# A hybrid decoder trunk on one core: the second token half's attention scores as three rounded products instead of one fp32 product

## The chip, the cores and the metric

The kernel runs on one core of one Trainium2 chip. A core has a matrix engine (PE; its weight loads are listed apart as PEld), a vector engine (DVE), an activation engine (ACT), a general engine (POOL), a queue engine (SP) and 16 DMA engines. Operands lie in SBUF, 128 partitions wide; matrix products land in PSUM, here in tiles of 128 x 512 fp32. The metric is the device time of one execution in microseconds. Three runs of the kernel before gave 992.62, 994.24 and 994.83 us, median 994.24.

## The reference

One sequence of 256 tokens, model width 2048, two layers. The first is a Mamba-2 mixer, the second an attention mixer; each is followed by `x = layernorm(alpha * x + mixer(x))`. The change lies in the second one, cut here to what matters:

```python
proj = x @ w_in                                   # [q | gate], each 2048 wide
q = (proj[..., :Q_WIDTH] + q_bias)                # 4 key-value heads x 8 query heads x 64
q = rope_partial(q, cos, sin)                     # first 16 of 64 dimensions
s = einsum("bcqhrd,bckhd->bchrqk", qb, kk) * (64 ** -0.5)
s = where(valid, s, -inf)                         # causal, window of 128
m = maximum(max(s), sink)
p = exp(s - m); p = p / (sum(p) + exp(sink - m))
o = einsum("bchrqk,bckhd->bcqhrd", p, vv) * silu(gate)
return o @ w_out
```

All inputs are fp32. With a window of 128, the first 128 tokens look at 128 keys, the second 128 tokens at 256. Keys and values are projected once, from the first layer's output.

## The kernel before, in words

**Products.** Nearly every product is made of three. A value a is split into a rounded part aH (type fp32r, which PE multiplies in one pass) and a remainder aL = a - aH; a product a b is then aH bH + aL bH + aH bL, summed in PSUM. For weights, ACT makes the rounded part (`wh`, L143) and DVE the remainder (`wl`, L144) of each half unit of 128 x 1024 that SP's queue has brought in (`wr`, L132). A unit is 128 x 2048 weights; PE spends 24 products of 512 columns or 48 of 256 on one. A few small products are plain fp32: among them the attention scores, L994.

**The first layer** (up to about 657 us) has its order written by hand. The change does not touch it.

**The attention layer** is written without a fixed order: a planner puts each engine's instructions into a queue by their place in the program and by when it reckons their inputs to be ready. On the chip, each engine then goes through its queue in order. The units come in the order `B_ORDER`: for each key-value head j a query block of four units (`q_block`, PE lines L881 to L883) and a gate block of four (`gate_block`, L269 to L271), later with the output blocks (`out_unit`, L330 to L332) between them. Small steps of attention are put off by a count of units with `later(n, fn)` and run by `tick()`.

For one head j the steps are these, h being the token half:

- `q_block` (L920): PE projects; DVE adds the bias row (L931) and rotates the first dimensions (`rope`, L862); DVE turns 32 x 32 blocks (L936), POOL's DMA queue writes them to DRAM and reads them back turned (`qd`, `qr`, L977 and L943).
- `scale_q` (L945): ACT copies the turned queries to `qT`, times 0.125.
- `attend` (L983): PE makes the scores L994, in fp32. Head dimension is 64, so two query heads use the two row halves of the PE array (rows 0 to 63 and 64 to 127), each into a PSUM tile of its own. For h = 0 there are 128 keys and two PSUM tiles, for h = 1 256 keys and four, of the four that the tag `ax` has. DVE takes the first half's scores out of PSUM (L1007); for the second half ACT copies and DVE fills in (L1002, L1003). Then come maximum, exponentials, sum and division (L1011 to L1022).
- `turn_p`, `load_p`: DVE turns the probabilities (L1028), POOL's queue writes and reads them (`pd`, `pT`). `mask_p` (L1042): for h = 1, DVE makes a masked copy `pm`. `pv` (L1048): PE multiplies with the values (L1052), DVE gates (`o`, L1059), ACT and DVE split the result (`oH` L1068, `oL` L1069).

The second half of head j follows one unit behind its first half. The masked copy of head j - 1, the query copy of head j and the scores of head j follow one another within some three units.

```python
for what, j in B_ORDER[:-1]:
    if what == "q":
        q_block(j)
        later(6, lambda j=j: attend(j, 0))
    elif what == "g":
        gate_block(j)
    else: ...
```

Of the kernel before, what the change touches and what calls it, by code (L numbers as in the profile page):

```python
# [8 lines left out]
F32 = mybir.dt.float32  # L9
F32R = mybir.dt.float32r  # L10
I32 = mybir.dt.int32
AF = mybir.ActivationFunctionType
ALU = mybir.AluOpType
AX = mybir.AxisListType

P = 128
S = 256
# [45 lines left out]
def trunk(ctx: ExitStack, tc: tile.TileContext, A: dict, out: bass.AP, dbg=None):  # L63
    nc = tc.nc
    PSUM = bass.MemoryType.PSUM

    def pool(name, bufs=1, side=None, space=None, stack=ctx):
        kw = {"space": space} if space is not None else {}
        return stack.enter_context(
            tc.tile_pool(name=name, bufs=bufs, side=side, reuse_waits="tile", **kw)  # L70
        )
# [9 lines left out]
    def nm(s):  # L81
        uid[0] += 1
        return f"{s}_{uid[0]}"

    def mm_tile():
        return mm_ps.tile([P, 512], F32, tag="mm", name=nm("mm"), bufs=4)
# [175 lines left out]
    def next_unit():  # L262
        used[0] += 1
        fill_units()
        flush()
        return units[used[0] - 1]
# [8 lines left out]
    def later(n, fn):  # L275
        pending.append([n, fn])
# [482 lines left out]
    for g in range(NG):  # L759
        t = 10 * g  # L760
# [92 lines left out]
    bp = pool("bp")  # L853
# [1 line left out]
    nc.gpsimd.dma_start(snk, A["snk"].partition_broadcast(P))  # L855

    def bias_row(src):
        t = bp.tile([P, 512], F32, tag="bias", name=nm("bias"), bufs=2)
        nc.gpsimd.dma_start(t[:], src.partition_broadcast(P))
        return t  # L860

    def rope(v, h, n):  # L862

        c = cs[:, h : h + 1, :].to_broadcast([P, n, 8])
        s = sn[:, h : h + 1, :].to_broadcast([P, n, 8])
        t = bp.tile([P, 4, 8, 8], F32, tag="rt", name=nm("rt"), bufs=1)
        x1, x2 = v[:, :, 0:8], v[:, :, 8:16]
        a, b, d, e = [t[:, i, :n, :] for i in range(4)]
        nc.vector.tensor_tensor(a, x1, c, ALU.mult)
        nc.vector.tensor_tensor(b, x2, s, ALU.mult)  # L870
        nc.vector.tensor_tensor(d, x2, c, ALU.mult)
        nc.vector.tensor_tensor(e, x1, s, ALU.mult)
        nc.vector.tensor_tensor(x1, a, b, ALU.subtract)
        nc.vector.tensor_tensor(x2, d, e, ALU.add)

    def x_stat(ps, h, u, ui):
        for k in range(4):
# [8 lines left out]
    kT = bp.tile([P, 4, S], F32, tag="kT", name="kT")  # L886
# [3 lines left out]
    for h in range(2):  # L890
        ps = mm_tile()
        for ui in range(4):
            if h == 0:
                kv_u.append(next_unit())
            x_stat(ps, h, kv_u[ui], ui)
        kd = bp.tile([P, 4, 2, 64], F32, tag="qt", name=nm("kd"), bufs=2)
        nc.vector.tensor_tensor(
            kd[:, :, 0, :], ps[:, :256].rearrange("p (j d) -> p j d", j=4),
            kvb[:, :256].rearrange("p (j d) -> p j d", j=4), ALU.add,
        )  # L900
        nc.vector.tensor_tensor(vt[:, h, :], ps[:, 256:], kvb[:, 256:], ALU.add)
        rope(kd[:, :, 0, :], h, 4)
        nc.gpsimd.tensor_copy(kd[:, :, 1, :], kd[:, :, 0, :])

        def ktr(h=h, kd=kd):
            pt = ax_tile()
            for j in range(4):
                nc.tensor.transpose(
                    pt[:, j * P : (j + 1) * P], kd[:, j, :, :].rearrange("p a d -> p (a d)"), ident
                )  # L910
            nc.scalar.copy(kT[:, :, h * P : (h + 1) * P], pt[:].rearrange("p (j t) -> p j t", j=4))

        later(2, ktr)
    nc.vector.tensor_tensor(vt[:, 1, :], vt[:, 1, :], vt[:, 0, :], ALU.subtract)

    qT = {}
# [3 lines left out]
    def q_block(j):  # L920
        pss = [mm_tile(), mm_tile()]
        qb = bias_row(A["qb"][j * 512 : (j + 1) * 512])
        for ui in range(4):
            u = next_unit()
            for h in range(2):
                x_stat(pss[h], h, u, ui)
            tick()
        for h in range(2):
            qt = bp.tile([P, 8, 64], F32, tag="qt", name=nm("qt"), bufs=2)
            qf = qt[:].rearrange("p a d -> p (a d)")  # L930
            nc.vector.tensor_tensor(qf, pss[h][:], qb[:], ALU.add)  # L931
            rope(qt[:], h, 8)

            def turn_q(h=h, qf=qf):
                z = bp.tile([P, 1024], F32, tag="pb", name=nm("zq"), bufs=5)[:, :512]
                nc.vector.transpose(  # L936
                    z.rearrange("p (c a t) -> p a c t", c=4, a=4), qf.rearrange("p (a c d) -> p a c d", a=4, c=4)
                )
                d = to_dram(z, 128, "qd")

                def load_q():
                    t = bp.tile([P, 8, 4, 32], F32, tag="pb", name=nm("qr"), bufs=5)[:, :4]
                    nc.gpsimd.dma_start(t.rearrange("p b a t -> p b (a t)"), d[:].rearrange("b p f -> p b f"))  # L943

                    def scale_q():  # L945
                        q2 = bp.tile([P, 4, P], F32, tag="qT", name=nm("qT"), bufs=2)
                        nc.scalar.activation(
                            q2[:].rearrange("p a (b t) -> p a b t", b=4), t.rearrange("p b a t -> p a b t"),
                            AF.Copy, scale=0.125,
                        )  # L950
                        qT[j, h] = q2

                    later(4, scale_q)

                later(1, load_q)

            turn_q()
# [25 lines left out]
    def attend(j, h):  # L983

        q2 = qT[j, h]
        p = bp.tile([P, 8, P], F32, tag="pb", name=nm("p"), bufs=5)
        nk = P * (h + 1)
        per = 512 // nk
        for b in range(0, 4, per):
            pss = [ax_tile(), ax_tile()]  # L990
            for i in range(per):
                for par in range(2):
                    rows = slice(64 * par, 64 * par + 64)
                    nc.tensor.matmul(  # L994
                        pss[par][:, i * nk : (i + 1) * nk], q2[rows, b + i, :], kT[rows, j, :nk],
                        start=True, stop=True,
                    )
            for par in range(2):
                v = p[:, par * 4 + b : par * 4 + b + per, :]
                sv = pss[par][:].rearrange("p (a k) -> p a k", a=per)  # L1000
                if h:
                    nc.scalar.copy(v, sv[:, :, P:])  # L1002
                    nc.vector.copy_predicated(  # L1003
                        v, mask_a0.bitcast(I32).unsqueeze(1).to_broadcast([P, per, P]), sv[:, :, :P]
                    )
                else:
                    nc.vector.tensor_tensor(v, sv, mask_a0.unsqueeze(1).to_broadcast([P, per, P]), ALU.add)  # L1007
# [92 lines left out]
    def done2(h):  # L1100
        mv, rs = norm_scale(bp, st2, h)
        if h:

            dg = bp.tile([P, P], F32, tag="dg", name="dg")
            pss = [ax_tile(), ax_tile()]
            for c in range(2):
                sl = slice(c * 512, (c + 1) * 512)
                nc.tensor.matmul(pss[c][:], ones[0:1, :], gb2[1][0:1, sl], start=True, stop=False)
            nc.scalar.activation(dg[:], ident, AF.Copy, scale=rs[:])
            for c in range(4):  # L1110
                sl = slice(c * 512, (c + 1) * 512)
                v = xr[:, h, sl]
                o = out[h * P : (h + 1) * P, sl]
                t = bp.tile([P, 512], F32, tag=("qt", "qT")[c % 2], name=nm("t"), bufs=2)
                nc.vector.scalar_tensor_tensor(  # L1115
                    t[:], v, mv[:, 0:1], gb2[0][:, sl], ALU.subtract, ALU.mult
                )
                if c < 2:
                    nc.tensor.matmul(pss[c][:], dg[:], t[:], start=False, stop=True)
                    nc.scalar.copy(v, pss[c][:])  # L1120
                    nc.scalar.dma_start(o, v)
                else:
                    nc.vector.scalar_tensor_tensor(v, t[:], rs[:], gb2[1][:, sl], ALU.mult, ALU.add)  # L1123
                    nc.sync.dma_start(o, v)
            return
        for c in range(4):
            sl = slice(c * 512, (c + 1) * 512)
            v = xr[:, h, sl]
            t = bp.tile([P, 512], F32, tag=("qt", "qT")[c % 2], name=nm("t"), bufs=2)
            nc.vector.scalar_tensor_tensor(  # L1130
                t[:], v, mv[:, 0:1], gb2[0][:, sl], ALU.subtract, ALU.mult
            )
            nc.scalar.activation(t[:], t[:], AF.Copy, scale=rs[:])
            nc.gpsimd.tensor_tensor(v, t[:], gb2[1][:, sl], ALU.add)
            nc.sync.dma_start(out[h * P : (h + 1) * P, sl], v)
# [96 lines left out]
```

## Time and profile before

| | |
|---|---|
| median of three runs | 994.24 us |
| the profiled execution | 993.8 us |
| its span, first to last instruction | 992.0 us |
| PE busy | 979.9 us, 99% |
| DVE, ACT, POOL busy | 791.1, 532.1, 171.2 us |
| attention scores L994, 256 keys | 64 instructions, 9.1 us busy |
| attention scores L994, 128 keys | 64 instructions, 4.6 us busy |
| mean clock granted to PE | 0.999 |

Rows of a timeline give the start within the span, the duration, the engine, the line, the operation, the tiles written and read, their shape and how many instructions were merged into the row; in brackets stands how long the engine was idle before and who released it. PE's instructions overlap, so the distance from start to start tells what one costs, not its duration. A row of the list of groups gives a line's operation with its count, busy time and mean duration in ns, and the idle time before it.

### The profile page before, as it was taken

To read this page: it belongs to the slowest core of one execution; us is meant where nothing else is said; L and a number is where in the kernel's file an instruction comes from. 1 tells how busy PE (TensorE), PEld (TensorE's weight loads), DVE (VectorE), ACT (ScalarE), POOL (GpSimd) and SP (SyncE) were. 2 spreads that over 40 slices of the span, in tenths; PEclk is the share of its full clock that TensorE was granted. 3 is DMA by queue.
4 is the path that set the end of the run, shared out by engine and by line. 5 is a ranking of instruction groups with operands and counts; after the bars stand their busy time and mean duration, and the time that the engine had idled before them with its cause. 6 is when DMAs were issued, how large, how long until landed. Compare 5 with 4: busy or idle time off the path is not lost. (4 is left out here: it accounts for less than half of the span.)

```text
span 992.0 us, 17541 instructions
## 1 busy us (share of the span) xinstructions
PE 979.9 (99%) x6836; PEld 879.6 (89%) x6836; DVE 791.1 (80%) x1219; ACT 532.1 (54%) x901; POOL 171.2 (17%) x225
## 2 busy tenths in 40 slices
PE   9999999999999999999999999999999999999997
PEld 7999989999998998999999999877898888777975
DVE  6879887976988787796797698999657586888686
ACT  6686747445634835743744564444446455444632
POOL 0004004005036001200400400501202203030102
PEclk9999999999999999999999999999999999999999
DMA  9588885586585667658559558756774758594942
GB/s 361 186 262 282 245 301 154 179 296 186 173 286 190 211 188 252 195 187 310 158 174 311 173 171 257 238 163 211 224 232 134 292 171 297 166 298 141 324 153 86
DMA packets 69443, 218.72 MB, mean 220 GB/s; under 512 B 8096, under 2 KB 19632, under 8 KB 68592
## 3 DMA queue, kind: packets, MB, share of 16 engines
q1 hardware_dynamic: 63648, 198.95, 61.4%
q0 software_dynamic: 5424, 18.12, 5.5%
q8 instruction: 54, 0.88, 0.4%
q10 hardware_dynamic: 288, 0.52, 0.1%
q14 instruction: 29, 0.24, 0.1%
HBM read 205.37 MB, written 12.19 MB: 219 GB/s over the span
## 5 line engine op out<-in xcount | busy, mean ns | idle before, releaser
L144 DVE TENSOR_TENSOR wl<-wr,wh 128x1024 fp32r<-128x1024 f32 (+2 forms) x338 | 398.0, 1207 | 94.9 <-ACT wh L143 94.2
L143 ACT ACTIVATE wh<-wr 128x1024 fp32r<-128x1024 f32 (+2 forms) x338 | 328.6, 1012 | 193.5 <-PE mm L331 68.8
L269 PE MATMUL mm<-xH,wh 128*128 128x256 f32 x1280 | 355.6, 278 | 0.0
L270 PE MATMUL mm<-xL,wh 128*128 128x256 f32 x1280 | 354.7, 277 | 0.0
L271 PE MATMUL mm<-xH,wl 128*128 128x256 f32 x1280 | 354.3, 277 | 0.0
L269 PEld LDWEIGHTS mm<-xH,wh 128*128 128x128 f32 x1280 | 240.6, 188 | 3.5 <-ACT wh L168 1.9
L270 PEld LDWEIGHTS mm<-xL,wh 128*128 128x128 f32 x1280 | 240.7, 188 | 1.1
L271 PEld LDWEIGHTS mm<-xH,wl 128*128 128x128 f32 x1280 | 240.5, 188 | 0.1
L626 POOL TENSOR_TENSOR yz<-yz,z 128x256 f32<-128x256 f32 x32 | 33.3, 1062 | 439.5 <-DVE yz L620 371.0
L330 PE MATMUL mm<-wh,yH 128*128 128x512 f32 x256 | 101.3, 396 | 2.1 <-DVE xr L337 2.1
L331 PE MATMUL mm<-wh,yL 128*128 128x512 f32 x256 | 99.9, 390 | 0.0
L332 PE MATMUL mm<-wl,yH 128*128 128x512 f32 x256 | 99.7, 390 | 0.0
L457 DVE SCALAR_TENSOR_TENSOR cv<-mm,pc,cv 128x255 f32<-128x255 f32 x144 | 69.1, 480 | 15.3 <-ACT cv L455 11.9
L270 PE MATMUL mm<-x1L,wh 128*128 128x256 f32 x256 | 70.8, 276 | 0.0
L269 PE MATMUL mm<-x1H,wh 128*128 128x256 f32 x256 | 70.7, 276 | 0.0
L271 PE MATMUL mm<-x1H,wl 128*128 128x256 f32 x256 | 70.7, 276 | 0.0
L881 PE MATMUL mm<-wh,x1H 128*128 128x512 f32 x160 | 63.7, 398 | 0.0
L883 PE MATMUL mm<-wl,x1H 128*128 128x512 f32 x160 | 62.8, 392 | 0.2 <-DVE wl L144 0.2
L882 PE MATMUL mm<-wh,x1L 128*128 128x512 f32 x160 | 62.6, 392 | 0.2 <-DVE x1L L845 0.2
L455 ACT ACTIVATE cv<-mm,pc 128x256 f32<-128x256 f32 x48 | 26.8, 559 | 62.4 <-PE mm L271 62.4
L330 PEld LDWEIGHTS mm<-wh,yH 128*128 128x128 f32 x256 | 48.1, 188 | 12.8 <-DVE xr L337 2.5
L332 PEld LDWEIGHTS mm<-wl,yH 128*128 128x128 f32 x256 | 48.0, 188 | 10.1
(213 smaller groups left out, 1357.8 us busy)
## 6 DMA issues: line engine op xcount, KB each, us to landing
wr<-in_wa SPq DMA_DIRECT2D x154, 512.0 KB, 5.2
wr<-in_wo SPq DMA_DIRECT2D x64, 512.0 KB, 5.1
wr<-in_wq SPq DMA_DIRECT2D x32, 512.0 KB, 4.8
wr<-in_wg SPq DMA_DIRECT2D x32, 512.0 KB, 4.8
wr<-in_wb SPq DMA_DIRECT2D x32, 512.0 KB, 5.5
rb<-rscr SPq DMA_DIRECT2D x16, 512.0 KB, 6.0
el<-rscr SPq DMA_DIRECT2D x16, 256.0 KB, 7.3
wr<-in_wkv SPq DMA_DIRECT2D x8, 512.0 KB, 6.7
```

Source lines behind the costliest of these rows:

```text
L143: nc.scalar.activation(h[:, sl], raw, AF.Copy)
L144: nc.vector.tensor_tensor(l[:, sl], raw, h[:, sl].bitcast(F32), ALU.subtract)
L269: nc.tensor.matmul(ps, ah, bh, start=first, stop=False)
L270: nc.tensor.matmul(ps, ah, bl, start=False, stop=False)
L271: nc.tensor.matmul(ps, al, bh, start=False, stop=last)
L330: nc.tensor.matmul(ps[:], aH[:, k, hs], u.h[:, ks], start=k == 0, stop=False)
L331: nc.tensor.matmul(ps[:], aL[:, k, hs], u.h[:, ks], start=False, stop=False)
L332: nc.tensor.matmul(ps[:], aH[:, k, hs], u.l[:, ks], start=False, stop=k == 3)
L457: nc.vector.scalar_tensor_tensor(a[:, sft:], ps[:, : S - sft], w(3 - sft), a[:, sft:], ALU.mult, ALU.add)
L881: nc.tensor.matmul(ps[:], x1H[:, kk, hs], u.h[:, ks], start=kk == 0, stop=False)
L882: nc.tensor.matmul(ps[:], x1L[:, kk, hs], u.h[:, ks], start=False, stop=False)
L883: nc.tensor.matmul(ps[:], x1H[:, kk, hs], u.l[:, ks], start=False, stop=kk == KT - 1)
```

## The change

The scores of the second token half are made of three rounded products. For h = 1, `scale_q` makes a rounded copy of the queries on ACT (`qT`, now fp32r), their remainder on DVE (`qL`), a rounded copy of the head's keys on ACT (`kH`) and their remainder on DVE (`kL`). In `attend`, each former product becomes three (rounded by rounded, remainder by rounded, rounded by remainder), with the two row halves side by side in each. The first half's scores stay fp32. The factor 0.125 moves from the queries to the keys, where it goes with the copy `kT` out of PSUM.

To make room in SBUF, the bias rows have one buffer instead of two, the rotation needs two temporary pieces instead of four (and writes two products in place), and the last step's tile `dg` takes over the rotation's buffer.

```diff
     def bias_row(src):
-        t = bp.tile([P, 512], F32, tag="bias", name=nm("bias"), bufs=2)
+        t = bp.tile([P, 512], F32, tag="bias", name=nm("bias"), bufs=1)
...
-        t = bp.tile([P, 4, 8, 8], F32, tag="rt", name=nm("rt"), bufs=1)
+        t = bp.tile([P, 2, 8, 8], F32, tag="rt", name=nm("rt"), bufs=1)
...
+        a, b = [t[:, i, :n, :] for i in range(2)]
+        nc.vector.tensor_tensor(a, x2, s, ALU.mult)
+        nc.vector.tensor_tensor(b, x1, s, ALU.mult)
+        nc.vector.tensor_tensor(x1, x1, c, ALU.mult)
+        nc.vector.tensor_tensor(x2, x2, c, ALU.mult)
+        nc.vector.tensor_tensor(x1, x1, a, ALU.subtract)
+        nc.vector.tensor_tensor(x2, x2, b, ALU.add)
...
-            nc.scalar.copy(kT[:, :, h * P : (h + 1) * P], pt[:].rearrange("p (j t) -> p j t", j=4))
+            nc.scalar.activation(
+                kT[:, :, h * P : (h + 1) * P], pt[:].rearrange("p (j t) -> p j t", j=4), AF.Copy, scale=0.125
+            )
...
-                        q2 = bp.tile([P, 4, P], F32, tag="qT", name=nm("qT"), bufs=2)
-                        nc.scalar.activation(
-                            q2[:].rearrange("p a (b t) -> p a b t", b=4), t.rearrange("p b a t -> p a b t"),
-                            AF.Copy, scale=0.125,
-                        )
-                        qT[j, h] = q2
+                        tv = t.rearrange("p b a t -> p a b t")
+                        q2 = bp.tile([P, 4, P], F32R if h else F32, tag="qT", name=nm("qT"), bufs=2)
+                        qv = q2[:].rearrange("p a (b t) -> p a b t", b=4)
+                        nc.scalar.activation(qv, tv, AF.Copy)
+                        qT[j, h] = [q2]
+                        if h:
+                            ql = bp.tile([P, 4, P], F32R, tag="qL", name=nm("qL"), bufs=1)
+                            nc.vector.tensor_tensor(
+                                ql[:].rearrange("p a (b t) -> p a b t", b=4), tv, qv.bitcast(F32), ALU.subtract
+                            )
+                            kh = bp.tile([P, S], F32R, tag="kH", name=nm("kH"), bufs=1)
+                            kl = bp.tile([P, S], F32R, tag="kL", name=nm("kL"), bufs=1)
+                            nc.scalar.activation(kh[:], kT[:, j, :], AF.Copy)
+                            nc.vector.tensor_tensor(kl[:], kT[:, j, :], kh[:].bitcast(F32), ALU.subtract)
+                            qT[j, h] += [ql, kh, kl]
...
-                for par in range(2):
-                    rows = slice(64 * par, 64 * par + 64)
-                    nc.tensor.matmul(
-                        pss[par][:, i * nk : (i + 1) * nk], q2[rows, b + i, :], kT[rows, j, :nk],
-                        start=True, stop=True,
-                    )
+                terms = [(q2[0], q2[2]), (q2[1], q2[2]), (q2[0], q2[3])] if h else [(q2[0], kT[:, j, :])]
+                for n, (q, k) in enumerate(terms):
+                    for par in range(2):
+                        rows = slice(64 * par, 64 * par + 64)
+                        nc.tensor.matmul(
+                            pss[par][:, i * nk : (i + 1) * nk], q[rows, b + i, :], k[rows, :nk],
+                            start=n == 0, stop=n == len(terms) - 1,
+                        )
...
-            dg = bp.tile([P, P], F32, tag="dg", name="dg")
+            dg = bp.tile([P, P], F32, tag="rt", name="dg", bufs=1)
```

More of the change, by code (lines that the diff above doesn't have):

```diff
@@ L865, in rope @@
         s = sn[:, h : h + 1, :].to_broadcast([P, n, 8])
-        t = bp.tile([P, 4, 8, 8], F32, tag="rt", name=nm("rt"), bufs=1)
+        t = bp.tile([P, 2, 8, 8], F32, tag="rt", name=nm("rt"), bufs=1)
         x1, x2 = v[:, :, 0:8], v[:, :, 8:16]
[L868 to L874, printed above, removed]
+        a, b = [t[:, i, :n, :] for i in range(2)]
[5 more added lines that the diff above has]
+        nc.vector.tensor_tensor(x2, x2, b, ALU.add)
     def x_stat(ps, h, u, ui):
```

## The prediction

> **What bounds the kernel now.** I read the page first, for which engine is full.
>
> ```profile
> span 992.0 us, 17541 instructions
> PE 979.9 (99%) x6836; PEld 879.6 (89%) x6836; DVE 791.1 (80%) x1219; ACT 532.1 (54%) x901; POOL 171.2 (17%) x225
> ```
>
> PE is busy for 99% of the span, so a shorter product should shorten the span, unless PE itself waits for somebody. The profiled execution took 993.8 us, which is 1.8 more than its span and 0.4 under the median of 994.24. The sum is made against 993.8 and 0.4 is added at the end.
>
> Next I read PE's timeline (start, duration, line, tiles, count) around the scores L994 of key-value head 0: the first token half, then the second, with the product ahead and the one behind.
>
> ```profile
> 744.81 0.39 PE L883 MATMUL mm<-wl,x1H 128*128 128x512 f32 x1
> 745.13 1.16 PE L994 MATMUL ax<-kT,qT 64*128 64x128 f32 x16
> 746.22 0.50 PE L881 MATMUL mm<-wh,x1H 128*128 128x512 f32 x1
> ...
> 751.57 0.39 PE L883 MATMUL mm<-wl,x1H 128*128 128x512 f32 x1
> 751.89 2.00 PE L994 MATMUL ax<-kT,qT 64*128 64x256 f32 x16
> 753.82 0.50 PE L881 MATMUL mm<-wh,x1H 128*128 128x512 f32 x1
> ```
>
> Eight fp32 products show as sixteen instructions: each is two passes. They run in pairs, one per row half, so a group is eight pair-passes. From first start to the next line's start that is 1.93 us at 256 columns and 1.09 at 128. The difference, 0.84 over 8, is 0.105 us for 128 columns, so a 256-column pair-pass is 0.21 and a group has 1.93 - 8 x 0.21 = 0.25 us of its own (entry and exit).
>
> The same two rows for heads 1, 2 and 3 show that PE does wait:
>
> ```profile
> 802.12 2.00 PE L994 MATMUL ax<-kT,qT 64*128 64x256 f32 x16
> 804.05 0.50 PE L881 MATMUL mm<-wh,x1H 128*128 128x512 f32 x1
> ...
> 852.35 2.69 PE L994 MATMUL ax<-kT,qT 64*128 64x256 f32 x16
> 854.97 0.50 PE L881 MATMUL mm<-wh,x1H 128*128 128x512 f32 x1
> ...
> 889.80 0.47 PE L330 MATMUL mm<-wh,oH 128*128 128x512 f32 x1 [0.47 <-DVE xr L335]
> ...
> 904.05 2.42 PE L994 MATMUL ax<-kT,qT 64*128 64x256 f32 x16
> 906.40 0.50 PE L330 MATMUL mm<-wh,oH 128*128 128x512 f32 x1
> ...
> 942.99 0.39 PE L332 MATMUL mm<-wl,oH 128*128 128x512 f32 x1
> 944.32 0.50 PE L330 MATMUL mm<-wh,oH 128*128 128x512 f32 x1 [0.94 <-DVE sg L969]
> ```
>
> Head 1 takes 1.93 like head 0. Heads 2 and 3 take 2.62 and 2.35, which is 0.69 and 0.42 too long. PE stands again for 0.47 at 889.80 and 0.94 at 944.32, both times released by DVE. So I read DVE's timeline for what it does there: pm L1042 (the masked copy of the first probabilities, which waits for the transposed ones by DMA), p L1007 (the first half's scores taken out of PSUM) and the last release.
>
> ```profile
> 790.66 1.23 DVE L1042 TENSOR_TENSOR pm<-pT,cc 128x1024 f32<-128x1024 f32 x1 [7.79 <-DMA pT<-pd]
> 801.48 1.28 DVE L1007 TENSOR_TENSOR p<-ax,cc 128x512 f32<-128x512 f32 x2
> ...
> 841.88 1.23 DVE L1042 TENSOR_TENSOR pm<-pT,cc 128x1024 f32<-128x1024 f32 x1 [8.37 <-DMA pT<-pd]
> 852.58 1.28 DVE L1007 TENSOR_TENSOR p<-ax,cc 128x512 f32<-128x512 f32 x2
> ...
> 892.27 1.22 DVE L1042 TENSOR_TENSOR pm<-pT,cc 128x1024 f32<-128x1024 f32 x1 [0.88 <-DMA pT<-pd]
> 904.01 1.27 DVE L1007 TENSOR_TENSOR p<-ax,cc 128x512 f32<-128x512 f32 x2
> ...
> 941.58 1.22 DVE L1042 TENSOR_TENSOR pm<-pT,cc 128x1024 f32<-128x1024 f32 x1 [6.37 <-DMA pT<-pd]
> 943.85 0.41 DVE L969 SCALAR_TENSOR_TENSOR sg<-sg,mm 128x256 f32<-128x256 f32 x1
> ```
>
> This is a loop. pm stands at the head of DVE's queue until its DMA lands. Behind it DVE works without a pause (rows with no idle time noted) for 10.8, 10.7 and 11.7 us until L1007. From L1007 over softmax, transposition and the way through DRAM to the next pm it is 40.4, 39.7 and 37.6 us. Twice round is 51.2 and 50.4 us, while PE's second-half groups start 802.12 - 751.89 = 50.23 apart. The loop is as long as PE's own work or a little longer, and from head 2 on PE runs into it: all four accumulator tiles of the scores are full until L1007 has emptied two, at 853.86 for head 2, in the middle of that group.
>
> **The change part by part.** *Removed and added on PE.* A second-half group becomes 24 rounded products, 12 pairs. The nearest row for one rounded pass of 256 columns is the gate product:
>
> ```profile
> 760.12 0.28 PE L269 MATMUL mm<-x1H,wh 128*128 128x256 f32 x1
> ...
> 770.00 0.28 PE L269 MATMUL mm<-x1H,wh 128*128 128x256 f32 x1
> ```
>
> Between these starts lie 87 products: 9.88 / 87 = 0.114 us. A new group is 12 x 0.114 + 0.25 = 1.62 us, 0.31 less than 1.93; four groups make 1.2 us. The trace has no rounded product on half the rows, so bounds: at best 0.105 per pair (the 0.82 ns per column of an fp32 pair-pass, halved for rounding), 1.51 per group and 1.7 us in all; at worst the two halves do not overlap, 24 x 0.114 + 0.25 = 2.99, a loss of 1.06 per group and 4.2 us in all. I take 0.114 since the group at 745.13 gets 16 loads and 16 products on half rows through at (1.09 - 0.25) / 8 = 0.105 per pair, loads included. [...]
>
> *What of the 1.2 us arrives.* Head 0 gains 0.31 and nothing holds PE there. Head 1 then starts its group at 801.8 and would reach its second accumulator pair at about 802.6, when L1007 ends at 802.76: a wait of 0.2, a net lead of about 0.4. Head 2's second pair is bound to L1007's end at 853.86, so only the half of the group behind it is shorter: PE leaves 0.16 earlier and the lead before it has become waiting. At 889.80 PE waits for L335 on DVE, and the 0.16 is gone. Head 3 repeats this, and at 944.32 PE waits for L969 behind pm. A lead of PE does not move pm, whose chain runs over DVE, ACT and DMA from 747 us on. So nothing of the 1.2 us is left at 944.32, and behind it no scores follow.
>
> *Added on DVE and ACT.* Per head, DVE gets two subtractions, qL over 512 columns and kL over 256, and ACT a copy kH. The nearest DVE rows are these:
>
> ```profile
> L1069 DVE TENSOR_TENSOR oL<-o,oH 128x512 fp32r<-128x512 f32 x8 | 5.5, 682 | 0.0
> L914 DVE TENSOR_TENSOR vt<-vt 128x256 f32<-128x256 f32 x1 | 0.4, 415 | 0.0
> ```
>
> In a full queue successive starts are about 0.08 closer than durations (801.48: two of 0.68 in 1.28), so 0.60 + 0.34 = 0.94 us per head. Where they stand in DVE's queue decides. They need both query copies of ACT:
>
> ```profile
> 785.65 0.63 ACT L947 ACTIVATE qT<-qr 128x512 f32<-128x512 f32 x1 [0.68 <-DMA qr<-qd]
> ...
> 837.19 0.63 ACT L947 ACTIVATE qT<-qr 128x512 f32<-128x512 f32 x1 [0.65 <-DMA qr<-qd]
> ...
> 889.27 0.61 ACT L947 ACTIVATE qT<-qr 128x512 f32<-128x512 f32 x1
> ```
>
> Those end at 786.3, 837.8 and 889.9, that is 4.4, 4.1 and 2.4 us before pm starts, and the query DMAs are issued before pT's in POOL's queue:
>
> ```profile
> 776.53 0.55 POOL L859 DMA_DIRECT2D bias<-in_qb  x1
> ...
> 828.21 1.50 POOL L943 DMA_DIRECT2D qr<-qd  x2
> 835.16 0.75 POOL L1035 DMA_DIRECT2D pT<-pd  x1 [5.46 <-DMA pd<-z]
> ```
>
> If the planner queues them ahead of pm, DVE does them in the 7.8 and 8.4 us in which it stands idle (0.88 for head 3, which nearly covers them), at no cost. If it queues them behind pm, they cost 0.94 in the loop each time. I take the first, because queries land first. The other rows for this part:
>
> ```profile
> L911 ACT COPY kT<-ax x2: 567/579/591, 701.5 to 702.0; 128x512 f32<-128x512 f32 x2
> ```
> ```profile
> 747.20 1.28 DVE L1007 TENSOR_TENSOR p<-ax,cc 128x512 f32<-128x512 f32 x2
> ...
> 865.06 0.68 DVE L931 TENSOR_TENSOR qt<-mm,bias 128x512 f32<-128x512 f32 x1
> ```
> ```profile
> 847.48 0.63 ACT L1068 ACTIVATE oH<-o 128x512 fp32r<-128x512 f32 x1 [5.60 <-DVE o L1059]
> ```
>
> For head 0 there is no pm, and L1007 at 747.20 is far ahead of PE's group at 751.89. ACT's copy is shorter than the 0.63 of a query copy and falls before ACT's wait for o, 5.60 us at head 2.
>
> *Moved or shrunk, costed at nothing.* The factor 0.125 goes from the query copy to the key copy L911; both exist already, and keys are ready at 703, 42 us before the first scores. The rotary step has six vector operations before and after. The bias ring of one makes each row wait for the last use of the one before: the fourth row, issued at 776.53, moves to the end of the query block before its own, one whole block ahead of its use at 865.06. If POOL met it too early, pd and pT behind it would be late and with them pm, at worst by the length of a query block's last unit, some 5 us (eight products of 0.23 three times over); I hold that unlikely. The dg tile shares a tag that is long free.
>
> **Sum:** 993.8 - 1.2 + 1.2 (taken back by DVE's loop) + 0 = 993.8, or **994.2** against the median.
>
> **The rivals.**
> 1. *The subtractions stand behind pm* (slower). It decides from head 1 on. The loop gets 0.94 longer at heads 1, 2 and 3, and pm at 941.58 comes 2.8 later: 997.0. For: pm is written before them in the program, so it has precedence when both are ready. Against: their input lands first.
> 2. *PE's gain arrives* (faster). The planner orders the whole attention stage anew, and if L1007 and pm come a little earlier, the 1.2 us stand and up to 0.69 + 0.42 + 0.47 + 0.94 = 2.5 us of waits go too: 993.0 to 990.5, middle 991.7. For: all four waits hang on the order of one queue. Against: nothing in the change shortens the loop.
> 3. *The pairs do not overlap, or load too slowly* (the change does not do what it says): 4.2 us lost on PE, of which the waits of 2.5 absorb most at heads 2 and 3; some 2 us arrive, 996.2.
>
> **How the numbers follow.** A measurement of this kernel tells a change of about 0.2%, 2.0 us, from none. Chances: forecast 0.40, its own range 993.0 to 995.4 (a head or so of either sign); rival 1 0.25; rival 2 0.25; rival 3 0.10. Of the forecast I count 0.32 as within 0.2% and 0.04 to each side, of rival 1 0.18 as slower, of rival 2 0.18 as faster, of rival 3 0.06 as slower, the rest as the same: faster 0.22, the same 0.50, slower 0.28. The range is 991.2 to 997.2: it takes in rival 1 in full, rival 3's likely outcome and more than half of rival 2.
>
> **What would show it.** Right: second-half groups of 24 products starting 0.11 apart per pair (about 1.6 us at head 0); longer waits of PE at heads 2 and 3 and at the place of 944.32; kL and qL on DVE before pm with idle time still ahead of pm; pm at the same times within 0.5 us. Wrong: pairs 0.2 apart (rival 3); kL and qL between pm and L1007, pm later by about 0.9 at each head (rival 1); or PE's waits gone (rival 2). The prediction falls as a whole if the loop pm to pm is shorter than before.

## The result and the profile after

The changed kernel takes 989.97 us (median of 20 runs, 988.18 to 993.6) where the kernel before takes 994.17 beside it (20 runs, 991.76 to 995.77): a ratio of 0.9966 with a 95% interval of 0.9958 to 0.9974. The forecast was 994.2 with a range down to 991.2, so the time lies below the range.

The execution that was profiled took 993.6 us, the longest of the 20; it shows the order of the work, and its length is read with that in mind. The page's first lines:

```profile
span 991.8 us, 17619 instructions
PE 980.7 (99%) x6868; PEld 881.7 (89%) x6868; DVE 795.7 (80%) x1227; ACT 534.5 (54%) x905; POOL 170.1 (17%) x225
```

PE is as full as before, so again the reading is in PE's few waits. PE's timeline (start, duration, line, operation, tiles, count, idle time) at the second-half groups of heads 2 and 3 and at the place where it waited last in the kernel before; the scores now have line 1007:

```profile
850.60 0.39 PE L1007 MATMUL ax<-kH,qT 64*128 64x256 f32 x2
850.83 0.28 PE L1007 MATMUL ax<-kH,qL 64*128 64x256 f32 x2
...
852.01 0.28 PE L1007 MATMUL ax<-kL,qT 64*128 64x256 f32 x2
852.22 0.50 PE L881 MATMUL mm<-wh,x1H 128*128 128x512 f32 x1
...
901.35 0.38 PE L1007 MATMUL ax<-kH,qT 64*128 64x256 f32 x1
901.95 0.38 PE L1007 MATMUL ax<-kH,qT 64*128 64x256 f32 x1 [0.22 <-DVE p L1020]
...
941.78 0.50 PE L330 MATMUL mm<-wh,oH 128*128 128x512 f32 x1 [1.95 <-DVE sg L980]
...
942.78 0.63 PE L330 MATMUL mm<-wh,oH 128*128 128x512 f32 x1
943.20 0.63 PE L331 MATMUL mm<-wh,oL 128*128 128x512 f32 x1
```

A group is 1.62 us from 850.60 to 852.22, and its pairs start (852.01 - 850.83) / 10 = 0.118 us apart. The group of head 2, which had been 2.62 us long, holds no wait any more. Two waits are left, 0.83 us in head 3's group and 1.95 us at 941.78, and behind the second one the products follow every 0.42 us instead of every 0.227.

DVE's timeline at the loop that held PE up: qL L955, the gate's last value sg L980, pm L1055, and the taking out of the first half's scores, L1020.

```profile
784.31 0.69 DVE L955 TENSOR_TENSOR qL<-qr,qT 128x512 fp32r<-128x512 f32 x1 [3.54 <-ACT qT L951]
785.26 1.22 DVE L144 TENSOR_TENSOR wl<-wr,wh 128x1024 fp32r<-128x1024 f32 x1 [0.26 <-PE mm L882]
786.40 0.41 DVE L980 SCALAR_TENSOR_TENSOR sg<-sg,mm 128x256 f32<-128x256 f32 x1
788.54 1.23 DVE L1055 TENSOR_TENSOR pm<-pT,cc 128x1024 f32<-128x1024 f32 x1 [1.72 <-DMA pT<-pd]
...
797.90 1.28 DVE L1020 TENSOR_TENSOR p<-ax,cc 128x512 f32<-128x512 f32 x2
...
837.93 1.23 DVE L1055 TENSOR_TENSOR pm<-pT,cc 128x1024 f32<-128x1024 f32 x1 [0.79 <-DVE sg L980]
...
847.15 1.28 DVE L1020 TENSOR_TENSOR p<-ax,cc 128x512 f32<-128x512 f32 x2
```

And the same place in the kernel before, directly behind pm at 790.66:

```profile
791.80 0.41 DVE L969 SCALAR_TENSOR_TENSOR sg<-sg,mm 128x256 f32<-128x256 f32 x1
792.13 2.56 DVE L144 TENSOR_TENSOR wl<-wr,wh 128x1024 fp32r<-128x1024 f32 x3
```

This is the difference. In the kernel before, sg and one full weight remainder wl stand behind pm, so they wait for pm's DMA and are then in the way of the scores. In the changed kernel both stand ahead of pm and are done while DVE would have stood idle. From pm to L1020 it is now 9.36 us at 797.90 and 9.22 at 847.15, instead of 10.8 and 10.7; at head 3 it is 10.01 instead of 11.7, since an output sum xr and a wl have changed sides in the same way. Taken out are 0.33 + 1.14 us each time, or 0.60 + 1.14, by the starts of these instructions.

The subtraction qL stands ahead of pm too, as forecast, in idle time. The new order was not written by anybody: the planner laid DVE's queue out anew when the products changed (with the same edits and one fp32 product it keeps the old order, e5 below).

Only the part behind pm is shorter at all three places. From pm to pm it is 49.4, 52.7 and 48.4 us in this profile, where the kernel before has 51.2, 50.4 and 49.3: behind L1020 of head 2 the probabilities are written and read back later (43.5 us to the next pm instead of 39.7), which leaves the wait of 0.83 us at head 3.

### The profile page after: what moved, and what is told of

Its sections match the earlier page's. It is cut to its first block, busy times and chain, and to the rows that moved or that the text cites. A ratio compares the mean times of both kernels' runs of the same rounds, so it can differ in the third digit from the quotient of the medians.

```text
span 991.8 us, 17619 instructions
## 1 busy us (share of the span) xinstructions
PE 980.7 (99%) x6868; PEld 881.7 (89%) x6868; DVE 795.7 (80%) x1227; ACT 534.5 (54%) x905; POOL 170.1 (17%) x225
## 4 chain that ended last, share of the span: by engine, by line
PE 78%; DVE 11%; ACT 4%; DMA 4%; issue 3%; POOL 0%; DVEq 0%; SPq 0%; POOLq 0%; ACTq 0%
PE mm L269 14%; PE mm L270 14%; PE mm L271 14%; PE mm L330 7%; PE mm L331 7%; PE mm L332 7%; PE mm L881 3%; DVE wl L144 3%; PE mm L882 3%; PE mm L883 3%; PE ax L609 2%; ACT wh L143 1%; DMA pd<-z 1%; PE ax L1007 1%; DMA gb<-in_lng 1%
## 5 line engine op out<-in xcount | busy, mean ns | idle before, releaser
L457 DVE SCALAR_TENSOR_TENSOR cv<-mm,pc,cv 128x255 f32<-128x255 f32 x144 | 69.2, 481 | 15.3 <-ACT cv L455 11.8
```

What stands on the lines that cost most here:

```text
L457: nc.vector.scalar_tensor_tensor(a[:, sft:], ps[:, : S - sft], w(3 - sft), a[:, sft:], ALU.mult, ALU.add)
```

## The experiments

All times are medians, ratios are against the kernel before on the same chip, where its median was 994.17 us (the changed kernel's row), 993.45 (e1, e2, e3, e5), 993.81 (e4, e6, e7, e9) or 993.86 (e8, e12, e13, e15). A ratio is estimated with its interval from all the runs and can differ from the quotient of two medians by 0.001 (e1: 991.40 / 993.45 is 0.9979). Times on different chips are compared by their ratios. The third column is worked out from each profiled execution: from the start of the first score group of head 0 to the start of the product behind the second-half group of head 3. There is no other change to PE's work in that stretch than the scores themselves, so it shows what waits and products do, and in e13 and at its end in e5 also what a lower clock does (last section).

| kernel | median, us | ratio (95%) | score stretch, us |
|---|---|---|---|
| before | 994.17 | 1 | 161.27 |
| changed | 989.97 | 0.9966 (0.9958 to 0.9974) | 158.77 |
| e6 changed, again | 989.31 | 0.9960 (0.9947 to 0.9973) | 157.94 |
| e1 before, new order at three heads | 991.40 | 0.9970 (0.9958 to 0.9983) | 159.40 |
| e2 before, new order at four heads | 990.18 | 0.9966 (0.9953 to 0.9978) | 159.31 |
| e7 changed, old order at heads 1, 2 | 992.28 | 0.9986 (0.9974 to 0.9998) | 159.91 |
| e5 changed, but fp32 scores | 996.76 | 1.0031 (1.0014 to 1.0047) | 163.71 |
| e3 changed, pm of the last head pinned | 989.11 | 0.9951 (0.9937 to 0.9964) | 157.93 |
| e15 fp32 scores, new order | 990.38 | 0.9968 (0.9956 to 0.9979) | 159.31 |
| e9 one product only | 989.21 | 0.9953 (0.9934 to 0.9971) | 157.61 |
| e4 side edits alone | 996.16 | 1.0021 (1.0005 to 1.0038) | 163.31 |
| e12 rotary step alone | 994.26 | 1.0011 (0.9994 to 1.0027) | 163.30 |
| e13 side edits without it | 994.79 | 1.0009 (0.9996 to 1.0022) | 163.51 |
| e8 changed, qL behind pm | 991.51 | 0.9976 (0.9961 to 0.9991) | 160.02 |

### The order without the products (e1, e2)

The kernel before, with an order-only dependence that puts pm behind the gate's value sg in DVE's queue; the planner then moves the weight remainder ahead as well. e1 does it for heads 0 to 2, e2 for all four.

```diff
-                nc.vector.tensor_tensor(
+                pm = nc.vector.tensor_tensor(
                     m[:], t[:], ...
                 )
+                tc.add_manual_dep(pm.ins, last["sg"].ins.name, NoSync)   # e1: if j < 3
```

> The kernel before, scores in fp32 as they were; only the order of DVE's queue is changed: the masked copy pm of heads 0, 1 and 2 is queued behind the gate step sg (and the remainder wl) that stood right behind it, as the planner has it in the changed kernel. Theory A (the gain came from the order: pm to L1007 gets 1.6 us shorter, and PE's waits for L1007 go): PE's 0.69 at head 2, 0.42 at head 3 and 0.47 at 889.80 are gone or halved, 1 to 1.6 us faster, 0.9985. Theory B (the gain came from the shorter products alone): no change, 1.000.

> As e1_order, with pm behind sg at the last head too, where PE waited 0.94 us for sg at 944.32. Theory A: 2 to 2.5 us faster than before, 0.9977, and 0.9 us faster than e1_order. Theory B: no change for heads 0 to 2, and at most the 0.94 of the last wait, 0.999.

DVE's timeline of e2 at head 0, then PE's at head 3's second-half group:

```profile
788.41 0.41 DVE L971 SCALAR_TENSOR_TENSOR sg<-sg,mm 128x256 f32<-128x256 f32 x1
790.45 1.22 DVE L1044 TENSOR_TENSOR pm<-pT,cc 128x1024 f32<-128x1024 f32 x1 [1.62 <-DMA pT<-pd]
...
799.81 1.28 DVE L1009 TENSOR_TENSOR p<-ax,cc 128x512 f32<-128x512 f32 x2
```
```profile
901.51 2.00 PE L996 MATMUL ax<-kT,qT 64*128 64x256 f32 x16
903.44 0.50 PE L330 MATMUL mm<-wh,oH 128*128 128x512 f32 x1
```

From pm to the scores it is 9.36 us, just as in the changed kernel. Behind the third pm the dependence moves nothing: it stays 11.75 us to the scores in e1 and e2. PE's groups in e2 are nevertheless 1.93 us long at every head (2.02 at head 3 in e1): the 0.69, 0.42 and 0.47 us that PE stood in the kernel before are gone or nearly so. The 0.94 behind pm of the last head is gone in the profiles of both, so without the dependence there too. With the products untouched, the order of two instructions at two places gives 0.9970 and, with the last head, 0.9966; the intervals don't tell these apart, and both gains are larger than the 0.9985 and 0.9977 expected. The stretch is 1.96 us shorter in e2. This is the theory that the prediction had turned down: DVE's queue order shortens the loop.

### The products with the old order (e7)

The changed kernel, with pm held ahead of sg and of one weight remainder again at heads 1 and 2 by the same kind of dependence the other way round.

```diff
-        later(6, mask_p)
+        later(5 if j < 2 else 6, mask_p)
...
+    tc.add_manual_dep(sg_value.ins, pm.ins.name, NoSync)   # likewise for one wl
```

> The changed kernel with its three rounded products, but at heads 1 and 2 the masked copy pm stands again ahead of the gate's last value sg and of a weight remainder wl on DVE, as in the kernel before (13 and 11 instructions from pm to the taking out of the first half's scores, instead of 11 and 9). Theory A (the order of DVE's queue brought the gain, and PE's shorter products alone are eaten by waits): 993 to 994.5 against 993.5 to 994.2 of the kernel before, ratio 0.999 to 1.001; pm to the end of the taking out 10.8 and 10.7 us again at those heads, second-half groups of heads 2 and 3 longer than 1.62 us by 0.4 or more, PE waits behind pm. Theory B (the shorter products brought the gain): 989.5 to 991, ratio 0.9955 to 0.997, and second-half groups of 1.62 us with little waiting.

DVE's timeline at head 2, then PE's in that head's group:

```profile
840.84 1.23 DVE L1072 TENSOR_TENSOR pm<-pT,cc 128x1024 f32<-128x1024 f32 x1 [3.41 <-DMA pT<-pd]
841.99 0.42 DVE L991 SCALAR_TENSOR_TENSOR sg<-sg,mm 128x256 f32<-128x256 f32 x1
842.32 3.49 DVE L145 TENSOR_TENSOR wl<-wr,wh 128x1024 fp32r<-128x1024 f32 x3
...
851.54 1.28 DVE L1037 TENSOR_TENSOR p<-ax,cc 128x512 f32<-128x512 f32 x2
```
```profile
852.27 0.38 PE L1024 MATMUL ax<-kH,qT 64*128 64x256 f32 x1
852.87 0.38 PE L1024 MATMUL ax<-kH,qT 64*128 64x256 f32 x1 [0.22 <-DVE p L1037]
```

pm to the scores takes 10.7 us again, and PE's wait in the group of head 2 is back: the group takes 2.33 us, that of head 3 2.63. With the shorter products in place two thirds of the gain are gone: 0.9986 against e6's 0.9960 on the same chip, just under the 0.999 to 1.001 that the order theory had expected and far from the 0.9955 to 0.997 of the other. The rest fits the two things that were left as in the changed kernel: the products, and the order behind the third pm (10.0 us to the scores instead of 11.7).

### The products by themselves (e5, e3, e15, e9)

e5 makes the rounded parts and remainders, but multiplies once in fp32, with the rounded queries. e3 is the changed kernel with pm of the last head held behind sg. e15 is e5 with pm held behind sg at all heads and queued as in e3. e9 is e3 with the two remainder products left out of the computation.

```diff
-terms = [(q2[0], q2[2]), (q2[1], q2[2]), (q2[0], q2[3])] if h else [(q2[0], kT[:, j, :])]
+terms = [(q2[0].bitcast(F32), kT[:, j, :])] if h else [(q2[0], kT[:, j, :])]   # e5, e15
+terms = [(q2[0], q2[2])] if h else [(q2[0], kT[:, j, :])]                       # e9
```

> The changed kernel with qL, kH and kL still made, but the second half's scores as one fp32 product of the rounded queries and the keys, so PE's groups are as long as before (the remainder of the queries is left out of the scores). The order around pm is then that of before: 13 and 11 instructions between pm and L1007 at heads 1 and 2. Theory A: no gain, 0.999 to 1.001, with PE's waits at heads 2 and 3 as before; the added work on DVE and ACT costs under 0.5 us since it stands ahead of pm. Theory B: no gain either. A loss of 1 us or more would say that the added work is not hidden.

> The changed kernel with one order changed: at the last head, pm is queued behind sg. The changed kernel's trace shows PE waiting 1.95 us for sg at 941.78 and then half the granted clock for some 3.6 us. Both theories say the lead that PE won is held up there; if nothing else is late behind it, 2 us faster than the changed kernel, or 3 to 3.5 where the lower clock goes with the wait: 986.5 to 988 us, 0.993. If the lead is held up again by the next thing (pv behind pm, or the last products behind their weights), no better than the changed kernel, 0.9966.

> The changed kernel with DVE's order around pm as in the pinned changed kernel (12, 10 and 14 instructions from pm to the taking out of the next first half's scores, and pm of the last head behind sg), but with one fp32 product for the second half's scores instead of three rounded ones; rounded parts and remainders are made all the same. It asks what the shorter products bring once DVE's order lets PE work. Theory A (what PE saves now counts in full): 4 x 0.31 us over the pinned changed kernel's 989.1, so 990 to 991.5, ratio 0.9965 to 0.998; second-half groups 1.93 us, next to no waits at heads 2 and 3. Theory B (the shorter products carried the gain): 993 or more, ratio 0.999 to 1.003, with PE's waits back at heads 2 and 3.

> The changed kernel with pm behind sg at the last head too, and with only the product of the two rounded parts for the second half's scores; both products with a remainder are left out of the computation (the remainders are still made). PE has 4 groups of 4 pairs, 0.71 us instead of 1.62, so 3.6 us less work. Theory A (with DVE's order mended PE is the bound, so its work counts in full): 985 to 986.2, that is 3 to 3.8 under the 989.1 of the same kernel with three products, ratio 0.991 to 0.992. Rival (another loop, over DVE, ACT and the transfers, is as long as PE's work by now, so PE's lead is taken back by waits): 988 to 989.5, with waits of PE at heads 2 and 3 of 0.5 us or more.

e5 came out at 1.0031, slower than the kernel before. With the one fp32 product the planner left pm ahead of sg (10.8, 10.7 and 11.8 us from pm to the scores), and the gain isn't there. By its expectation a loss of over 1 us would say that the added work is not hidden. The trace speaks against that: qL and kL stand ahead of pm with 2.9 to 5.0 us of idle time left. The side edits without the split lose 1.0021 by themselves (e4, next part), and the intervals don't tell the two kernels apart, so what the rest of the loss is stays open. PE waited 1.21 us in the group of head 3. e15 and e3 have the same times from pm to the scores (9.36, 9.22 and 10.0) and no wait of PE in the scores. PE's timeline of head 3's group in e15, then in e3:

```profile
900.85 2.00 PE L1009 MATMUL ax<-kT,qT 64*128 64x256 f32 x16
902.78 0.50 PE L330 MATMUL mm<-wh,oH 128*128 128x512 f32 x1
```
```profile
901.10 0.38 PE L1009 MATMUL ax<-kH,qT 64*128 64x256 f32 x2
...
902.71 0.50 PE L330 MATMUL mm<-wh,oH 128*128 128x512 f32 x1
```

The groups are 1.93 and 1.61 us, and the stretch over four heads is 159.31 and 157.93: 1.38 us for the products, close to the 1.2 that the prediction had summed up. In time it is 990.38 against 989.11, 1.3 us; these were timed on different chips and their intervals overlap, so the shown size is that of the trace. e3 has the lowest median of this study, but its interval overlaps the changed kernel's. The 986.5 to 988 us expected of it were missed: the wait at the last head is gone, and it is gone in e6 without the dependence too.

e9 asks whether PE is now the bound. Its groups are 0.67 us where PE doesn't wait, 3.8 us less work in four heads than e3, and its median is the same. PE's timeline at head 3, then DVE's third pm and the scores behind it:

```profile
901.41 0.38 PE L1009 MATMUL ax<-kH,qT 64*128 64x256 f32 x1 [1.83 <-DVE p L1022]
902.01 0.70 PE L1009 MATMUL ax<-kH,qT 64*128 64x256 f32 x3 [0.21 <-DVE p L1022]
```
```profile
889.53 1.22 DVE L1057 TENSOR_TENSOR pm<-pT,cc 128x1024 f32<-128x1024 f32 x1 [4.58 <-DMA pT<-pd]
...
900.68 1.28 DVE L1022 TENSOR_TENSOR p<-ax,cc 128x512 f32<-128x512 f32 x2
```

Counted from its first score group, PE came 2.8 us earlier to this group than in e3 (153.5 us against 156.3), and it waited 2.0 for DVE. That is the rival's reading, for head 3 alone; at head 2 there is no wait. But the planner changed the queue once more: behind the third pm it is 11.15 us to the scores where e3 has 10.01, so by an estimate 1.1 of the 2.0 us come from the order, and e9 doesn't compare the products alone. The runs spread from 985.18 to 993.18. Three of them lie at or under 985.76, where theory A had put the median. The five shortest, up to 987.57, all had a mean granted clock of 0.996 or more; the four longest, from 991.12, had 0.992 or 0.993. By an estimate from these figures, 0.005 of 989 us is 10 us more at half the clock and up to 5 us lost, which is most of what lies between them (last section). So PE's gain arrives in some executions, and whether the loop holds it up in the others, with e3's order, stays open.

### The side edits (e4, e12, e13)

e4 has the bias ring of one, the rotary step in place, the shared tile and the factor 0.125 moved, with fp32 scores and no split. e12 has the rotary step alone on the kernel before, e13 has e4 with the old rotary step.

```diff
-        t = bp.tile([P, 512], F32, tag="bias", name=nm("bias"), bufs=2)
+        t = bp.tile([P, 512], F32, tag="bias", name=nm("bias"), bufs=1)            # e4, e13
...
-        nc.vector.tensor_tensor(x1, a, b, ALU.subtract)
+        nc.vector.tensor_tensor(x1, x1, c, ALU.mult)
+        nc.vector.tensor_tensor(x1, x1, a, ALU.subtract)                           # e4, e12
```

> The change without its products: only the bias ring of one, the rotary step in place, the shared tile of the diagonal and the factor 0.125 moved to the keys; the second half's scores are one product in fp32, and nothing is split. The order of DVE's queue around pm is that of the kernel before (13, 11 and 15 instructions). Theory A (order): no gain, ratio 0.999 to 1.001, PE's waits at heads 2 and 3 as before. Rival (the side edits carry some of the gain, as the first layer ended 1 us earlier in the profile of the changed kernel): ratio 0.997 to 0.999, with the first row of the attention stage 0.5 to 1 us earlier.

> The kernel before with one edit of the change: the rotary step in place, nothing else. Theory A (order of DVE's queue): the six small operations of the step now chain differently, and DVE's queue puts the last transposition of head 2's probabilities z behind one weight remainder more; the write pd of that head starts 1.2 to 1.7 us later after the taking out of the scores (24.7 instead of 23.5), PE waits longer at head 3, ratio 1.001 to 1.003. Rival (the step is neutral, as predicted: six operations before and after): ratio 0.999 to 1.001.

> The kernel before with the other side edits: the bias ring of one, the shared tile of the diagonal, the factor 0.125 moved to the keys; the rotary step as before, fp32 scores. DVE's order is that of the kernel before (z of head 2 not later, 13, 11 and 15 instructions around pm). Theory A (order): ratio 0.999 to 1.001. Rival (the moved bias row delays pd's landing): pd to the issue of pT 10 us or more at heads 1 and 2 where the kernel before has 9.1 and 8.8, ratio 1.001 to 1.003.

Both parts were expected to do nothing by the prediction. Together they cost 2 us (1.0021, the interval excludes 1), which neither reading of e4 had put; singly each is 1.0011 and 1.0009, which the intervals don't tell from 1. For the rotary step the trace shows a mechanism: DVE's timeline of e12 at head 2, then of the kernel before, where z L1028 is the transposition that the write of the probabilities waits for.

```profile
850.83 1.28 DVE L1007 TENSOR_TENSOR p<-ax,cc 128x512 f32<-128x512 f32 x2
...
872.25 1.22 DVE L144 TENSOR_TENSOR wl<-wr,wh 128x1024 fp32r<-128x1024 f32 x1
873.38 0.68 DVE L335 SCALAR_TENSOR_TENSOR xr<-xr,mm 128x512 f32<-128x512 f32 x1
873.98 1.24 DVE L1028 STREAM_TRANSPOSE z<-p 128x1024 f32<-128x1024 f32 x1
```
```profile
874.08 1.23 DVE L1028 STREAM_TRANSPOSE z<-p 128x1024 f32<-128x1024 f32 x1
875.23 1.18 DVE L144 TENSOR_TENSOR wl<-wr,wh 128x1024 fp32r<-128x1024 f32 x1
```

A wl that stood behind z now stands ahead of it: from the taking out of the scores to z it is 23.1 us in e12 and 21.5 in the kernel before (852.58 to 874.08). Part of this returns on POOL, which in the kernel before was still issuing the queries' writes when z was done (z ended at 875.31, they at 876.06): the write pd starts 24.7 us after the start of L1007 instead of 23.5. The write at head 2 is later by 1.2, and PE waited 1.21 us for the scores to be taken out in the group of head 3. The changed kernel has this order as well (24.7 us). What it costs there isn't shown: e15 has it too, with all the side edits, and its stretch is e2's, which has none of them (159.31 both).

For e13 the rival read that the moved bias row delays pd. From pd's issue to pT's it took 10.3 us at head 1 where the kernel before has 9.1, but 8.8 at head 2 in both, so what e13 costs, if anything, stays open. PE waited 1.14 us in the group of head 2:

```profile
853.55 1.72 PE L997 MATMUL ax<-kT,qT 64*128 64x256 f32 x8 [1.14 <-DVE p L1010]
```

### The subtraction behind pm (e8) and a second profile (e6)

e8 holds qL behind pm in the changed kernel, as in the first rival; e6 is the changed kernel itself.

```diff
+    tc.add_manual_dep(ql_subtract.ins, pm.ins.name, NoSync)   # e8
```

> The changed kernel with the subtraction qL held behind pm on DVE at each head (the first rival's order, with kL left early). Theory A (the loop over DVE sets PE's waits): 0.60 us more between pm and the taking out of the scores at heads 1, 2 and 3 (9.96, 9.82 and 10.6 us); the changed kernel has about 1 us of slack in that loop at heads 1 and 2 and none at head 3, so PE waits 0.3 to 1.2 us more in all: 990 to 991.5, ratio 0.9965 to 0.998. Rival (there is slack enough): 989.5 to 990, ratio 0.9955 to 0.9965, PE's groups unchanged.

> The changed kernel itself, unaltered, beside the others on one chip. Theory A and B: 989.5 to 990.5, ratio 0.9958 to 0.9974. Of its profile: if the stretch of half clock behind the wait of 1.95 us at 941.78 is a consequence of that wait, it is there again whenever PE waits about 2 us there (some 1.8 us lost); if it was chance, the wait is there without it, and the span is under 990.

DVE's timeline of e8 at head 2, then PE's in the group of head 3:

```profile
840.10 1.22 DVE L1062 TENSOR_TENSOR pm<-pT,cc 128x1024 f32<-128x1024 f32 x1 [1.76 <-issue]
841.24 0.68 DVE L956 TENSOR_TENSOR qL<-qr,qT 128x512 fp32r<-128x512 f32 x1
...
849.92 1.27 DVE L1027 TENSOR_TENSOR p<-ax,cc 128x512 f32<-128x512 f32 x2
```
```profile
903.62 0.38 PE L1014 MATMUL ax<-kH,qT 64*128 64x256 f32 x1 [1.23 <-DVE p L1027]
```

pm to the scores is 9.82 us, 0.60 more as worked out, and PE waits 1.45 us at head 3 (1.23 and 0.22) where e6 has no wait; at most 1.2 had been expected. The ratio, 0.9976, is where the order theory had put it; its interval overlaps that of the changed kernel, so the loss is shown by the wait and not by the time alone. In e6 the stretch is 157.94 with no wait at head 3 or behind the last pm, which started at 937.29; there the transfer of pT took 6.5 us from issue to pm where the first profile has 9.0 (930.03 to 939.03). The wait of 1.95 at 941.78 came with that late transfer. As e6 has no wait there, it doesn't say whether the half pace behind it belongs to it; the other traces, and another wait in e6, say more (last section).

## Why the prediction was wrong

**What held.** The loop over DVE as the holder of PE (e1, e2, e7 and e8 move it by known amounts and PE's waits follow). The product: 0.114 per pair forecast, 0.118 measured, 1.62 us per group forecast and measured. Loads of the two row halves overlap: at 850.71 in the changed kernel both loads of a pair are listed in one row of 0.19 us, as long as the row of a single load (0.19 at 852.22), and the next pair's start 0.118 later. The subtractions, in idle time ahead of pm at no cost, with 0.60 as the price behind it (e8).

**What failed** is one step: "nothing in the change shortens the loop", and with it the sum's third term, 1.2 us "taken back by DVE's loop". The parts of the loop were read off as 10.8, 10.7 and 11.7 us and carried over as if DVE's queue were fixed. They became 9.36, 9.22 and 10.01, and with fp32 products e2 gains 3.3 us by two of these alone and the last head's order. From pm to pm, the prediction's own sign for falling as a whole, the loop is shorter in the first turn (49.4 instead of 51.2) and longer in the second (52.7 instead of 50.4). That the planner might order the stage anew stood as the second rival at a quarter; it should have stood higher, since the kernel's front part says that the queues of this layer are laid out by when the planner reckons inputs to be ready, and the change alters products, operations and buffers in that layer. The prices of that rival were near: 1.2 us of product (1.3 measured) and 2.5 us of waits, 990.5 at its best, with 989.97 measured. The order gave more than those waits (3.3 us in e2, 2.2 to 4.7 by its interval).

**A second step failed the other way.** "Moved or shrunk, costed at nothing": the side edits cost 2 us by themselves (e4), through the same queue, and six operations before and six after were no proof of the contrary. The answer came out lower than the forecast as the new order around pm outweighs it, or removes it: with that order no cost of them is seen (e15 beside e2).

**The sum as the runs have it**, from the kernel before: the order around pm gives 3.3 us with fp32 products (e2, 993.45 to 990.18 on its chip); the products add 1.3 (e15 to e3, 1.38 in the trace). That makes 4.6, against 4.2 measured, with an uncertainty of over 1 us in each; the changed kernel lacks the last head's dependence, which e2, e3 and e15 have. Of e2's 3.3 us the score stretch shows 1.96 and the wait at 944.32 another 0.94.

## What to carry to other kernels

Where a planner fills in-order queues, a change's largest effect may be a reordering of instructions that it doesn't name, so compare the queues of both versions around the instruction that waits for a transfer before pricing any product. Whatever is ready belongs ahead of such an instruction: here two instructions on the wrong side of pm were worth some 3 us (e2), and the shorter products 1.3. Shorten the bound engine and the loop behind it together: in e7 the shorter products, with the old order back at two heads, kept a third of the gain.

## What the runs showed of the hardware

**In some profiles PE's products ran at half pace behind a wait, and the length of the wait alone doesn't say in which.** Behind the 1.95 us wait of the changed kernel PE's products followed 0.42 us apart instead of 0.227. The changed kernel in three windows (stretch, length, busy time and count of PE, PEld, DVE, ACT and POOL, granted clock, DMA share, GB/s):

```profile
938.00:942.30 4.30, 2.35 (x11) 1.63 (x10) 3.27 (x4) 1.06 (x1) 0.00 (x0) 1.00 0.95 392
942.40:945.70 3.30, 3.30 (x9) 2.61 (x8) 3.30 (x5) 0.00 (x0) 0.00 (x0) 0.50 0.81 254
945.80:949.00 3.20, 3.20 (x15) 1.32 (x13) 3.20 (x5) 3.16 (x4) 0.00 (x0) 1.00 0.86 301
```

The granted clock is half for about 3.4 us (942.3 to 945.8), and full during the wait itself and after the stretch. The same stretch, with products 0.42 to 0.43 us apart, stands behind the waits of 1.14 us in e13 (855.5 to 858.9), 1.21 in e4, e5 and e12, 1.45 in e8 and 2.0 in e9. Each loses about 1.6 us more, an estimate from eight products 0.2 us further apart. The 0.69 and 0.94 us waits of the kernel before left no such stretch (granted clock 1.00 from 853.9 to 858.0 and from 944.3 to 948.0). But a longer wait didn't always leave one: every kernel here waits 1.7 to 2.2 us in the first layer, near 127 us. PE's row behind that wait and the window that follows, in the kernel before, then in e6:

```profile
128.02 0.50 PE L330 MATMUL mm<-wh,yH 128*128 128x512 f32 x1 [2.10 <-DVE xr L337]
```
```profile
129.00:132.00 3.00, 3.00 (x19) 2.63 (x19) 3.00 (x4) 0.54 (x2) 0.00 (x0) 1.00 0.81 275
```
```profile
127.34 0.50 PE L330 MATMUL mm<-wh,yH 128*128 128x512 f32 x1 [1.95 <-DVE xr L337]
```
```profile
129.00:132.00 3.00, 3.00 (x9) 2.37 (x8) 2.97 (x5) 1.11 (x2) 0.00 (x0) 0.50 0.86 283
```

In four of the fourteen profiles (e6, e7, e8, e9) the half clock follows this wait, in the other ten it doesn't. So part of the spread between runs of one kernel can come from a place that no edit touched; what decides it is not shown.

The four fp32 products at the very end stand behind a gap of 0.89 us in every profile; e2, then e3:

```profile
980.75 1.98 PE L1127 MATMUL ax<-t,dg 128*128 128x512 f32 x4 [0.89 <-ACT dg L1117]
```
```profile
979.98 3.56 PE L1140 MATMUL ax<-t,dg 128*128 128x512 f32 x4 [0.89 <-ACT dg L1130]
```

They took 1.98 us in five profiles (before, e1, e2, e5, e7) and 2.56 to 3.78 in the other nine, so the length of the gap doesn't decide it here either. The granted clock over them was 1.00 in the kernel before and 0.50 in the changed kernel (3.78 us), where it was 0.50 from 983.4 on, inside the gap.
